# Two rests of the weights' split placed behind each chunk's shared results in VectorE's order

## Chip, cores and metric

The kernel runs on one core of a Trainium2 chip, in one launch. The metric is device time in microseconds (us), as the median of several runs. All shares and stamps below come from one profiled execution of the kernel before; its timeline counts from the start of its span.

## What is computed

Two layers of a residual trunk over an input x of 1 x 256 x 2048 in float32. Cut to what matters here:

```python
for l in range(2):
    h = rms_norm(x, pre_mix_norm[l])
    m = hybrid_mixer(h, ...)            # h @ w_in, 8 stick-breaking and 8 differential heads, @ w_o
    x = x + rms_norm(m, post_mix_norm[l])
    h = rms_norm(x, pre_ffn_norm[l])
    f = (silu(h @ w_gate[l]) * (h @ w_up[l])) @ w_down[l]   # 2048 -> 5632 -> 2048
    x = x + rms_norm(f, post_ffn_norm[l])
```

All weights are float32, and the output is compared at float32 accuracy.

## The kernel before

**Weights.** All weights are read once, in one order that is fixed on the host (`weights_in_turn`), as tiles of 128 x 1024 float32 (two blocks of 128 rows by 512 columns, 512 KB). To keep float32 accuracy with TensorE's faster 32-bit type, each tile is split: ScalarE writes a rounded copy `hi` (L271), VectorE writes the rest `lo = raw - hi` (L273), and every product is three matmuls, hi x hi, lo x hi, hi x lo (`product`, L976 to L978; the activations are split in the same way). In this text a *rest* is the operation on L273. `raw` tiles lie in a ring of 4 (L214), `hi` and `lo` in rings of 6. `feed` (L261) issues the split of the tiles in stream order, LOOKAHEAD = 4 tiles ahead of the product that uses them; `fetch` issues their loads on SP's queue, some tiles further ahead. A load into `raw` has to wait until the rest that read that slot four raw tiles earlier is done.

**Sevens.** Some pairs of weight tiles go through a seven-product scheme (as Strassen and Winograd's) instead of eight products: `seven_products` (L993). They need sums of weight blocks, made in `mixed_weights` (L229): the two tiles arrive as G and T (T with an accumulating second transfer issued from POOL, L224), T and G are combined on VectorE (L252, L253), and split on ScalarE (L245) and VectorE (L246) into hi, lo, Th and Tl. Four of the seven products are added into the output banks directly; four PSUM banks, p1, p6, p7 and q5, hold sums that several outputs share.

**Shared results.** After the last seven of a chunk, `shared_part` turns the four extra banks into four tiles, with one copy on ScalarE and four operations on VectorE:

```python
nc.scalar.copy(w[0], p1)                                                   # L1013
nc.vector.tensor_tensor(out=w[1], in0=p6, in1=w[0], op=ALU.subtract)       # L1014
nc.vector.tensor_tensor(out=w[2], in0=p7, in1=w[1], op=ALU.add)            # L1015
nc.vector.tensor_tensor(out=w[1], in0=q5, in1=w[1], op=ALU.add)            # L1016
nc.vector.tensor_tensor(out=w[3], in0=q5, in1=w[2], op=ALU.add)            # L1017
```

It is called in the input projection (L924), the output projection (L1066), gate and up (L1147) and down (L1242).

**Gate and up** (L1125 to L1166). 11 chunks of 512 columns in each layer; a chunk runs over 8 pairs of k blocks (kp) and adds into four banks c11, c12, c21, c22 (token half by gate or up). Four kps of a chunk are sevens (2, 4, 5, 6), but only two in chunk 0 (4, 6) and three in chunk 1 (4, 5, 6). In chunks 0 and 1 of each layer the sums of activations for later sevens are formed too (`pair_sums`, the f tiles of L1105, and `token_sums`, s, sh and sl, L983 to L990). The eight PSUM banks are two sets of four: the extra banks of a chunk are the output banks of the next one. So the first matmuls of chunk c + 1 into c11 to c22 must wait until the shared results of chunk c have read p1, p6, p7 and q5. At a chunk's end the banks are combined with the shared results and gated (L1152, L1153 silu on ScalarE, L1154, L1155), and the result is transposed on PE and copied back by ScalarE (L1161, L1162) some matmuls later.

**Down** (L1176 to L1270) runs in two halves of 1024 columns over 22 kps, seven of them sevens in each half; each half has one shared part. The last three kps of half 1 are done token half by token half.

**Order.** Engines run their queues in program order. The order of each queue is decided when the kernel is built, by a scheduler that places instructions by their dependencies and modelled readiness. `tc.issue_after(x)` adds an edge of order to it: what is issued inside stands behind x on the same engine. It adds no semaphore. Engines synchronise through semaphores on the tiles they share.

Of the kernel before, what the change touches and what calls it, by code (L numbers as in the profile page):

```python
# [2 lines left out]

# [6 lines left out]
F32 = mybir.dt.float32  # L10
# [3 lines left out]
ALU = mybir.AluOpType  # L14
# [7 lines left out]
NT = S // P  # L22
# [37 lines left out]
def gate_sevens(c):  # L60

    return (FIRST_SEVEN, NEXT_SEVEN)[c] if c < 2 else SEVEN
# [89 lines left out]
def kernel(  # L152
# [15 lines left out]
    nc = tc.nc  # L168
# [14 lines left out]
    def four_banks(odd, names):  # L183
        makers = (bank, bank, bank, last_bank) if odd else (acc_bank,) * 4
        return [make(n) for make, n in zip(makers, names)]
# [9 lines left out]
    def fetch(upto):  # L195
        while len(raws) < min(upto, len(stream)):
            i = len(raws)
            for j in range(i, min(i + EARLY + 1, mix_raw[3])):
                if j in sevens and j not in sums:
                    summed(j)  # L200
            if i in sevens:
                raws.append(sums[i])
                continue
            if i + 1 in sevens:
                g = mix_raw[0].tile([P, 2, CW], F32, tag="G", bufs=mix_raw[1], name=f"G{i}")
                loads.append(nc.sync.dma_start(g, stream[i]))
                raws.append(g)
                continue
            if i in own or i + 1 in own:
                raw = mix_pool[0].tile([P, 2, CW], F32, tag="v", bufs=2, name=f"V{i}")  # L210
            elif i in plain or i + 1 in plain:
                raw = mix_pool[0].tile([P, 2, CW], F32, tag="GU", bufs=4, name=f"GU{i}")
            else:
                raw = wpool.tile([P, 2, CW], F32, tag="raw", bufs=4, name=f"raw{i}")  # L214
            loads.append(nc.sync.dma_start(raw, stream[i]))
            raws.append(raw)
# [44 lines left out]
    def feed(upto):  # L261
        fetch(upto)
        while fed[0] < min(upto, len(stream)):
            i = fed[0]
            raw = raws[i]
            if i in sevens or i in plain or i in own:
                ready[i] = mixed_weights(i)
                fed[0] += 1
                continue
            hi = wpool.tile([P, 2, CW], F32R, tag="hi", bufs=6, name=f"hi{i}")  # L270
            nc.scalar.activation(hi, raw, AF.Copy)  # L271
            lo = wpool.tile([P, 2, CW], F32R, tag="lo", bufs=6, name=f"lo{i}")
            rest = nc.vector.tensor_tensor(out=lo, in0=raw, in1=hi.bitcast(F32), op=ALU.subtract)  # L273
            ready[i] = (hi, lo)
            fed[0] += 1
            rests.append(rest)

    rests = []

    def after_rests():  # L280

        return tc.issue_after(rests[-1].ins)
# [5 lines left out]
    def weights(i, ahead):  # L288
        feed(i + 1 + ahead)
        return ready[i]  # L290
# [175 lines left out]
    def start(gen, n=1):  # L466
        running.append([clock[0] + n, gen])
# [542 lines left out]
    def shared_part(extra, w):  # L1010

        p1, p6, p7, q5 = extra
        nc.scalar.copy(w[0], p1)  # L1013
        nc.vector.tensor_tensor(out=w[1], in0=p6, in1=w[0], op=ALU.subtract)  # L1014
        nc.vector.tensor_tensor(out=w[2], in0=p7, in1=w[1], op=ALU.add)  # L1015
        nc.vector.tensor_tensor(out=w[1], in0=q5, in1=w[1], op=ALU.add)  # L1016
        nc.vector.tensor_tensor(out=w[3], in0=q5, in1=w[2], op=ALU.add)  # L1017

    def shared_sign(t, col):
        return ALU.subtract if (t, col) == (1, 0) else ALU.add  # L1020
# [2 lines left out]
    for l in range(L):  # L1023
# [11 lines left out]
        mg = {}  # L1035
# [16 lines left out]
        for kp in LATE_O:  # L1052
            i, j = (plan[l]["o"][c, kp] for c in (2, 3))
# [4 lines left out]
            if kp == O_SEVEN[0]:  # L1058
                extra = four_banks(False, [f"{q}_o{l}" for q in ("p1", "p6", "p7", "q5")])
            hi, lo = weights(i, LOOKAHEAD)  # L1060
# [47 lines left out]
        def eight(banks, c, kp, toks, first, last):  # L1108
            g, u = weights(plan[l]["gate"][c, kp], LOOKAHEAD), weights(plan[l]["up"][c, kp], LOOKAHEAD)
            for kk in range(2):  # L1110
                st = xT[2 * kp + kk]
                for t in toks:
                    tick()
                    stat = (st[:, 0, t * P : (t + 1) * P], st[:, 1, t * P : (t + 1) * P])
                    for col, (hi, lo) in enumerate((g, u)):
                        product(banks[2 * t + col], stat, (hi[:, kk, :], lo[:, kk, :]), first and kk == 0, last and kk == 1)
# [8 lines left out]
        for c in range(FF // CW):  # L1125
            banks = four_banks(1 - c % 2, [f"c{q}_{l}_{c}" for q in ("11", "12", "21", "22")])
            mine = gate_sevens(c)
            order = FIRST_ORDER if c == 0 else tuple(range(KT // 2))
            if c == 0:
                for t in range(NT):  # L1130
                    for kp in order[:2]:
                        eight(banks, c, kp, (t,), kp == order[0], False)
                order = order[2:]
            extra = None
            for n, kp in enumerate(order):
                if (c, n) in FORM_AT:
                    with after_rests():
                        pair_sums(FORM_AT[c, n])
                if kp not in mine:
                    eight(banks, c, kp, range(NT), kp == 0, kp == order[-1])  # L1140
                    continue
                if kp == mine[0]:
                    extra = four_banks(c % 2, [f"{q}_{l}_{c}" for q in ("p1", "p6", "p7", "q5")])
                seven(banks, extra, c, kp, kp == mine[0], kp == mine[-1])
                if kp == mine[-1]:
                    w = [pool.tile([P, CW], F32, tag="t2", name=f"w{j}_{l}_{c}") for j in range(4)]
                    shared_part(extra, w)  # L1147
            at = pool.tile([P, 4, S], F32, tag="act", bufs=FF // CW, name=f"act{l}_{c}")
            act.append(at)
            sg = [w[0], w[2]]  # L1150
            for t, u in ((0, w[1]), (1, w[3])):
                nc.vector.tensor_tensor(out=sg[t], in0=banks[2 * t], in1=sg[t], op=shared_sign(t, 0))  # L1152
                nc.scalar.activation(sg[t], sg[t], AF.Silu, scale=rs[t][:, 0:1])  # L1153
                nc.vector.tensor_tensor(out=u, in0=banks[2 * t + 1], in1=u, op=ALU.add)  # L1154
                nc.vector.scalar_tensor_tensor(out=sg[t], in0=u, scalar=rs[t][:, 0:1], in1=sg[t], op0=ALU.mult, op1=ALU.mult)  # L1155

            def flip(sg=sg, at=at, c=c):
                for t in range(NT):
                    pb = (acc_bank if c % 2 else bank)(f"actT_ps{l}_{c}_{t}")
                    for j in range(4):  # L1160
                        nc.tensor.transpose(pb[:, j * P : (j + 1) * P], sg[t][:, j * P : (j + 1) * P], ident)  # L1161
                    nc.scalar.copy(at[:, :, t * P : (t + 1) * P], pb.rearrange("p (k q) -> p k q", k=4))  # L1162
                    yield 1

            start(flip(), DEFER_ACT)
# [7 lines left out]
        mg = {}  # L1173
        ssm = [small.tile([P, 4], F32, tag="ssm", name=f"ssm_d{l}_{t}") for t in range(NT)]
        nkp = FF // P // 2
        for half in range(2):  # L1176
# [48 lines left out]
            for kp in range(nkp - tail):  # L1225
                if half == 1 and kp == X_BACK:
                    back = [pool.tile([P, 4, S], F32, tag="act", bufs=FF // CW, name=f"xd{l}_{n}") for n in range(4)]
                    back = [b.rearrange("p k n -> p (k n)") for b in back]
                    xs[:] = [back[:2], back[2:]]
                    with in_turn():  # L1230
                        for t, h in ((0, 0), (0, 1), (1, 0), (1, 1)):
                            load_x(t, h, away[-1])
                if kp not in mine:
                    down(kp, range(NT))
                    continue
                if kp == mine[0]:
                    extra = four_banks(1 - half, [f"{q}_d{l}_{half}" for q in ("p1", "p6", "p7", "q5")])
                down_seven(kp)
                if kp == mine[-1]:
                    for t in range(NT):  # L1240
                        mg[t, half] = dn.tile([P, 2, CW], F32, tag="qk", bufs=4, name=f"mg_d{l}_{t}_{half}")
                    shared_part(extra, [mg[t, half][:, j, :] for t in range(NT) for j in range(2)])  # L1242
                    if open_sums[0]:
                        for c in cc:
                            nc.vector.tensor_tensor(out=accs[c, 1], in0=accs[c, 1], in1=mg[1, half][:, c % 2, :], op=shared_sign(1, c % 2))
# [5 lines left out]
            for t in range(NT):  # L1251
# [4 lines left out]
                for c in cc:  # L1256
                    for kp in range(nkp - tail, nkp):
# [3 lines left out]
                        hi, lo = weights(plan[l]["down"][c, kp], LOOKAHEAD)  # L1261
# [67 lines left out]
```

## Time and profile before

| what | value |
|---|---|
| runs | 2206.82, 2209.6, 2212.26 us; median 2209.6 us |
| profiled execution, own time | 2204.91 us |
| its span | 2203.2 us |
| granted TensorE clock | 0.999 |
| rests, L273 from raw | 522, 627.5 us busy, mean 1220 ns; idle before them 122.6 us, 121.4 of it put down to hi (L271) |
| hi, L271 from raw | 522, 541.1 us busy, mean 1053 ns; idle before them 234.8 us, 71.7 of it put down to the loads |
| loads of raw | 522 of 512 KB, 4.7 us median to landing |
| gate and up, from its first matmul to the first of down | 396.8 to 866.9 us in layer 0, 1493.4 to 1963.0 us in layer 1 |
| a steady gate and up chunk (6 to 7, layer 0) | 41.74 us |

The span runs from the first to the last instruction; the execution's own time is 1.7 us more. Busy shares are averages over the whole span, and stages differ. In a row of a timeline, the bracket at the end holds how long the engine stood idle before that instruction and what released it; idle time of an engine that nothing waits for costs nothing. PE stands for TensorE's matmuls, PEld for its weight loads, DVE for VectorE, ACT for ScalarE, POOL for GpSimd, SP for SyncE's queue of DMA issues.

### The profile page before, as it was taken

To read this page: it belongs to the slowest core of one execution; us is meant where nothing else is said; L and a number is where in the kernel's file an instruction comes from. 1 tells how busy PE (TensorE), PEld (TensorE's weight loads), DVE (VectorE), ACT (ScalarE), POOL (GpSimd) and SP (SyncE) were. 2 spreads that over 40 slices of the span, in tenths; PEclk is the share of its full clock that TensorE was granted. 3 is DMA by queue.
4 is the path that set the end of the run, shared out by engine and by line. 5 is a ranking of instruction groups with operands and counts; after the bars stand their busy time and mean duration, and the time that the engine had idled before them with its cause. 6 is when DMAs were issued, how large, how long until landed. Compare 5 with 4: busy or idle time off the path is not lost.

```text
span 2203.2 us, 28510 instructions
## 1 busy us (share of the span) xinstructions
PE 2180.6 (99%) x9991; PEld 1788.1 (81%) x9991; DVE 1902.2 (86%) x2609; ACT 1371.9 (62%) x2052; POOL 140.2 (6%) x186
## 2 busy tenths in 40 slices
PE   9999999999999999999999999999999999999998
PEld 7788888778888888888878888887788888888886
DVE  7888658899999999989888886579999999999897
ACT  7566665656656656666665666657566556566664
POOL 1200000000000000000011000000000000000000
PEclk9999999999999999999999999999999999999999
DMA  8654555776776675767465545658677677767683
GB/s 313 204 178 153 191 189 169 251 246 215 224 248 215 211 255 183 247 214 260 153 230 191 171 162 183 192 171 267 212 224 237 222 220 238 231 212 233 205 261 102
DMA packets 138512, 467.27 MB, mean 212 GB/s; under 512 B 15872, under 2 KB 16640, under 8 KB 137856
## 3 DMA queue, kind: packets, MB, share of 16 engines
q1 hardware_dynamic: 120656, 430.30, 56.5%
q0 software_dynamic: 15840, 28.84, 7.8%
q10 hardware_dynamic: 1872, 6.31, 0.8%
q8 instruction: 78, 1.28, 0.2%
q14 instruction: 66, 0.54, 0.1%
HBM read 457.00 MB, written 8.39 MB: 211 GB/s over the span
## 4 chain that ended last, share of the span: by engine, by line
PE 84%; DVE 9%; issue 2%; DMA 2%; ACT 2%; SPq 0%; DVEq 0%; ACTq 0%
PE c L976 8%; PE c L978 8%; PE c L977 8%; PE in L976 6%; PE in L978 6%; PE in L977 6%; PE dn L1212 4%; PE dn L1210 4%; PE dn L1209 4%; DVE lo L273 2%; PE p L977 2%; PE p L976 2%; PE p L978 2%; PE o L492 2%; PE o L493 2%
## 5 line engine op out<-in xcount | busy, mean ns | idle before, releaser
L273 DVE TENSOR_TENSOR lo<-raw,hi 128x1024 fp32r<-128x1024 f32 x522 | 627.5, 1220 | 122.6 <-ACT hi L271 121.4
L271 ACT ACTIVATE hi<-raw 128x1024 fp32r<-128x1024 f32 x522 | 541.1, 1053 | 234.8 <-DMA raw<-in_weights_in_turn_dram 71.7
L976 PE MATMUL c<-hi,xF 128*128 128x512 f32 x834 | 328.2, 396 | 3.5 <-DVE w L1017 1.6
L977 PE MATMUL c<-lo,xF 128*128 128x512 f32 x834 | 325.2, 390 | 0.5 <-DVE lo L273 0.5
L978 PE MATMUL c<-hi,xF 128*128 128x512 f32 x834 | 324.6, 390 | 0.0
L224 POOL DMA_DIRECT2D T<-in_weights_in_turn_dram x110 | 95.8, 874 | 1685.5 <-DMA T<-in_weights_in_turn_dram 596.5
L976 PEld LDWEIGHTS c<-hi,xF 128*128 128x128 f32 x834 | 156.3, 188 | 38.7 <-ACT hi L271 3.8
L977 PEld LDWEIGHTS c<-lo,xF 128*128 128x128 f32 x834 | 156.7, 188 | 33.5 <-DVE lo L273 2.7
L978 PEld LDWEIGHTS c<-hi,xF 128*128 128x128 f32 x834 | 156.6, 188 | 32.8
L1209 PE MATMUL dn<-hi,jh 128*128 128x512 f32 x432 | 168.3, 389 | 0.0
L1210 PE MATMUL dn<-lo,jh 128*128 128x512 f32 x432 | 168.1, 389 | 0.0
L273 DVE TENSOR_TENSOR lo<-G,hi 128x1024 fp32r<-128x1024 f32 x110 | 134.0, 1219 | 33.8 <-ACT hi L271 33.7
L245 ACT ACTIVATE Th<-G 128x1024 fp32r<-128x1024 f32 x110 | 116.0, 1055 | 40.2 <-DVE G L253 38.3
L246 DVE TENSOR_TENSOR Tl<-G,Th 128x1024 fp32r<-128x1024 f32 x110 | 134.0, 1218 | 5.3 <-ACT Th L245 5.3
L245 ACT ACTIVATE hi<-T 128x1024 fp32r<-128x1024 f32 x110 | 115.4, 1049 | 36.1 <-PE c L978 26.5
L246 DVE TENSOR_TENSOR lo<-T,hi 128x1024 fp32r<-128x1024 f32 x110 | 134.0, 1218 | 2.7 <-ACT hi L245 2.7
L253 DVE TENSOR_TENSOR G<-G,T 128x1024 f32<-128x1024 f32 x110 | 134.2, 1220 | 1.9
L1212 PE MATMUL dn<-hi,jl 128*128 128x512 f32 x432 | 133.0, 389 | 0.0
L245 ACT ACTIVATE Th<-T 128x512 fp32r<-128x512 f32 x110 | 68.9, 627 | 101.7 <-DVE T L252 85.5
L976 PE MATMUL in<-hi,xT 128*128 128x512 f32 x328 | 131.6, 402 | 0.0
L976 PE MATMUL in<-hi,xI 128*128 128x512 f32 x328 | 130.6, 401 | 0.0
L977 PE MATMUL in<-lo,xI 128*128 128x512 f32 x328 | 128.2, 391 | 1.5 <-DVE lo L273 1.5
(448 smaller groups left out, 4733.6 us busy)
## 6 DMA issues: line engine op xcount, KB each, us to landing
raw<-in_weights_in_turn_dram SPq DMA_DIRECT2D x522, 512.0 KB, 4.7
T<-in_weights_in_turn_dram SPq DMA_DIRECT2D x110, 512.0 KB, 4.5
G<-in_weights_in_turn_dram SPq DMA_DIRECT2D x110, 512.0 KB, 5.3
T<-in_weights_in_turn_dram POOLq DMA_DIRECT2D x110, 256.0 KB, 6.9
GU<-in_weights_in_turn_dram SPq DMA_DIRECT2D x32, 512.0 KB, 4.6
V<-in_weights_in_turn_dram SPq DMA_DIRECT2D x8, 512.0 KB, 3.9
away_ffn<-x ACTq DMA_DIRECT2D x8, 512.0 KB, 4.1
xd<-away_ffn SPq DMA_DIRECT2D x8, 512.0 KB, 8.1
```

What stands on the lines that cost most here:

```text
L224: nc.gpsimd.dma_start(sums[i][:, 0, :], stream[i - 1][:, 0, :], accum_op=ALU.add)
L245: nc.scalar.activation(h, w, AF.Copy)
L246: nc.vector.tensor_tensor(out=l, in0=w, in1=h.bitcast(F32), op=ALU.subtract)
L253: nc.vector.tensor_tensor(out=g, in0=g, in1=t2.unsqueeze(1).to_broadcast([P, 2, CW]), op=ALU.add)
L271: nc.scalar.activation(hi, raw, AF.Copy)
L273: rest = nc.vector.tensor_tensor(out=lo, in0=raw, in1=hi.bitcast(F32), op=ALU.subtract)
L976: nc.tensor.matmul(a, sh, hi, start=first, stop=False, skip_group_check=open_sums[0])
L977: nc.tensor.matmul(a, sh, lo, start=False, stop=False, skip_group_check=open_sums[0])
L978: nc.tensor.matmul(a, sl, hi, start=False, stop=last, skip_group_check=open_sums[0])
L1209: nc.tensor.matmul(accs[c, t], sh, hi[:, kk, :], start=first, stop=False, skip_group_check=open_sums[0])
L1210: nc.tensor.matmul(accs[c, t], sh, lo[:, kk, :], start=False, stop=False, skip_group_check=open_sums[0])
L1212: nc.tensor.matmul(accs[c, t], sl, hi[:, kk, :], start=False, stop=last, skip_group_check=open_sums[0])
```

## The change

`shared_part` returns its last operation on VectorE (w[3]). In gate and up and in down, that operation is kept together with a count of 2, and the next two rests that `feed` issues on plain raw or G tiles are put behind it by `tc.issue_after`. The calls in the input and the output projection keep nothing. There are 26 such places, 11 in each gate and up and 2 in each down.

```diff
-            rest = nc.vector.tensor_tensor(out=lo, in0=raw, in1=hi.bitcast(F32), op=ALU.subtract)
+            with behind():
+                rest = nc.vector.tensor_tensor(out=lo, in0=raw, in1=hi.bitcast(F32), op=ALU.subtract)
...
+    held = [None, 0]
+
+    def behind():
+
+        if held[1] == 0:
+            return nullcontext()
+        held[1] -= 1
+        return tc.issue_after(held[0].ins)
...
-        nc.vector.tensor_tensor(out=w[3], in0=q5, in1=w[2], op=ALU.add)
+        return nc.vector.tensor_tensor(out=w[3], in0=q5, in1=w[2], op=ALU.add)
...
-                    shared_part(extra, w)
+                    held[:] = shared_part(extra, w), 2
...
-                    shared_part(extra, [mg[t, half][:, j, :] for t in range(NT) for j in range(2)])
+                    held[:] = shared_part(extra, [mg[t, half][:, j, :] for t in range(NT) for j in range(2)]), 2
```

The lines of the changed kernel are shifted: the rests are on L274 and the shared results on L1022 to L1026 there, the end of a chunk on L1161 to L1164.

No instruction is added or removed on any engine. In a steady chunk VectorE's order is, before: rest, L1014, L1015, rest, L1016, L1017, L1152; after: L1014, L1015, L1016, L1017, rest, rest, L1152. Around it the scheduler places some other instructions differently: loads on SP's queue (a T load ahead of one raw load, a raw load ahead of one G load in each steady chunk), a few operations of ScalarE in chunks 0 and 1, the transposes of chunk 10 on PE (28 matmuls earlier), and, at the end of layer 1's down, six matmuls of another sum that now stand ahead of those whose rests are held.

More of the change, by code (lines that the diff above doesn't have):

```diff
@@ L1 @@
 import math
-from contextlib import ExitStack
+from contextlib import ExitStack, nullcontext
 import concourse.bass as bass
```

## Prediction

> **What bounds the kernel now.** I read the page's busy line first, then PE's waits in the gate and up stage, then stretches of 41 to 42 us, then VectorE's, ScalarE's and PE's timelines around the shared results.
>
> ```profile
> PE 2180.6 (99%) x9991; PEld 1788.1 (81%) x9991; DVE 1902.2 (86%) x2609; ACT 1371.9 (62%) x2052; POOL 140.2 (6%) x186
> ```
>
> PE is busy for 99% of the span; an edit on VectorE can only win where PE waits for it. The windows view (stretch and its length, then busy us of PE, PEld, DVE, ACT, POOL, then granted clock, DMA share, GB/s) shows where: chunks 0 to 1 and 1 to 2 of layer 0, and a steady chunk, 6 to 7.
>
> ```profile
> 444.00:485.00 41.00, 40.77 (x181) 32.82 (x180) 39.09 (x52) 24.84 (x30) 3.45 (x4) 1.00 0.72 221
> 485.00:527.00 42.00, 39.78 (x175) 31.65 (x175) 38.61 (x43) 26.35 (x30) 2.61 (x3) 1.00 0.74 226
> 652.06:693.80 41.74, 41.74 (x190) 34.58 (x189) 39.00 (x44) 25.35 (x29) 3.48 (x4) 1.00 0.73 233
> ```
>
> PE is never idle in the steady chunk; it is a little in the first two. The waits of PE from 436 to 530 us (us, times, longest):
>
> ```profile
> PE p L977 <- DVE Tl L246: 1.2, 3, 0.5
> PE c L976 <- DVE w L1017: 0.8, 1, 0.8
> PE c L976 <- DVE w L1015: 0.5, 1, 0.5
> PE p L976 <- ACT Th L245: 0.2, 1, 0.2
> ```
>
> The same view answers with no line at all for 530 to 862, 860 to 1085 and 1626 to 1958 us. For 1532 to 1626 (layer 1's first chunks) it gives nearly the same sum, 2.7 us. A wait also stretches the matmul behind it. Matmuls start 0.227 us apart when nothing is late; what the trace has over that is 4.7 us in 444 to 527 and 4.3 us in 1540 to 1623. So **9.0 us, 0.4% of the time, is all that the change can win in gate and up**.
>
> The place itself, chunk 1 to 2 of layer 0, on VectorE and ScalarE (start, duration, instruction, idle time before it and its releaser):
>
> ```profile
> 483.47 0.68 DVE L1014 TENSOR_TENSOR w<-p,w 128x512 f32<-128x512 f32 x1
> 487.86 1.23 DVE L273 TENSOR_TENSOR lo<-raw,hi 128x1024 fp32r<-128x1024 f32 x1 [3.71 <-ACT hi L271]
> 489.00 0.68 DVE L1015 TENSOR_TENSOR w<-p,w 128x512 f32<-128x512 f32 x1
> 489.61 0.68 DVE L1152 TENSOR_TENSOR w<-c,w 128x512 f32<-128x512 f32 x1
> 490.20 0.68 DVE L1016 TENSOR_TENSOR w<-q,w 128x512 f32<-128x512 f32 x1
> 490.80 0.68 DVE L1017 TENSOR_TENSOR w<-q,w 128x512 f32<-128x512 f32 x1
> 491.40 1.21 DVE L273 TENSOR_TENSOR lo<-raw,hi 128x1024 fp32r<-128x1024 f32 x1
> 492.53 0.68 DVE L1154 TENSOR_TENSOR w<-c,w 128x512 f32<-128x512 f32 x1
> ```
>
> ```profile
> 486.77 1.06 ACT L271 ACTIVATE hi<-raw 128x1024 fp32r<-128x1024 f32 x1 [7.66 <-DMA raw<-in_weights_in_turn_dram]
> 489.67 1.06 ACT L271 ACTIVATE hi<-raw 128x1024 fp32r<-128x1024 f32 x1 [1.84 <-DMA raw<-in_weights_in_turn_dram]
> ```
>
> The first rest stands ahead of L1015 and waits 3.71 us for a late raw tile. L1015 to L1017 stand behind it, and PE needs their banks: it waits at 489.74 for L1015, then for L1017, then for Tl:
>
> ```profile
> 491.53 0.50 PE L976 MATMUL c<-hi,xF 128*128 128x512 f32 x1 [0.81 <-DVE w L1017]
> 504.42 0.50 PE L977 MATMUL p<-Tl,sh 128*128 128x512 f32 x1 [0.54 <-DVE Tl L246]
> ```
>
> **The change, part by part.** No instruction is added or removed. 26 shared results (22 gate and up, 4 down) each hold two rests of 1.22 us (L273: 627.5 us over 522) behind the last of four operations of 0.68 us. Only orders move, as the lists of instructions of each engine show; no instruction waits on a further semaphore. What stands behind the two rests on VectorE is L1152 or L1154 of the chunk's end, and what waits for a rest is PE and, through the slot of its raw tile, SP's queue.
>
> *Steady chunks, 16 of them.* Before, one rest stands between w1 and w2's successors and waits 0.28 us for hi:
>
> ```profile
> 693.79 0.68 DVE L1014 TENSOR_TENSOR w<-p,w 128x512 f32<-128x512 f32 x1
> ...
> 709.08 1.22 DVE L246 TENSOR_TENSOR Tl<-G,Th 128x1024 fp32r<-128x1024 f32 x1
> 712.39 1.23 DVE L273 TENSOR_TENSOR lo<-G,hi 128x1024 fp32r<-128x1024 f32 x1 [2.08 <-ACT hi L271]
> ```
>
> p6 is complete at 693.27. After: L1014 at 693.33, L1015 694.05, L1016 694.77, L1017 to 696.05, the two rests to 698.25. L1152 stood at 698.07, so +0.18 us on VectorE, and the 2.08 us of idle time at 712 takes that up. PE uses the later rests' tiles from 705.58, 7 us after they end. Their raw slots come free up to 3.2 us later (697.1 for 693.87), but the tiles that load there landed at 700.73 and 703.17 and are first read at 724.72 and 726.28. Behind them on SP's queue one T load changes places with a raw load (708.06 and 707.46) and the next raw with a G (710.71 and 710.33): 0.6 us for tiles that are read over 10 us after they land. Sum 0; without that cover it would be 16 x 0.18 = 2.9 us. (The Trainium skill, Perfetto Trace Analysis, "Identifying the Most-Contended Engine", would judge TensorE by its weight loads, 81% here, and optimise the engine with the highest occupancy, which makes VectorE with 86% the bound. The trace disagrees: no PE wait from 530 to 862. As a rival it stands below.)
>
> *Chunk 0 to 1, layer 0.* Both rests move behind L1017 and the operations on f (L1105). L1015 to L1017 come about 0.9 us earlier, where PE didn't wait. The first rest ends at 448.1 instead of 445.3, so the load into its raw slot is issued 2.8 us later, at 448.1 (it took 5.35 us). PE waited at 457.46 (0.2 over) for a rest behind that load: hi 1.06, sh 0.61, sl 0.69 and the rest's own 1.22 are 3.6, with some 0.4 for the handovers 4.0, so 448.1 + t + 4.0. Break-even is t = 5.4 if PE is to stand as before, 5.2 to win the 0.2. The nearest raws took 4.33 (449.52) and 5.96 (436.91), mean 5.1: 457.2. I take -0.1; bounds -0.2 and (t = 5.96) +0.6.
>
> *Chunk 1 to 2, layer 0.* L1017 ends at 486.3 instead of 491.4, so PE's waits at 489.74 (0.61 over its spacing) and 491.53 (0.98) go. But the second rest still waits for its raw tile (hi at 489.67, DMA of 8.25 us): it runs 490.76 to 491.9, and L1154 starts at 492.5 as before. Everything behind on VectorE (Tl, for which PE waits at 504.42, 0.70 over, and at 526.21, 0.57) stands still, so PE, early by 1.6, waits there longer instead: what PE gains over the whole is what VectorE gains, and VectorE hangs on that DMA. I take 0; bounds 0 and -1.6.
>
> *Layer 1's first chunks.* The same two places. In chunk 0 to 1 the first rest (1539.88) leaves the front of L1015 and ends at about 1544.3 instead of 1541.1; the load behind it took 6.95 us. PE waited at 1554.17 (0.68 over): 1544.3 + t + 3.95 is 1553.35 with t = 5.1, so that wait goes, -0.7; with 6.95 it is 1555.2, +1.0. In chunk 1 to 2 the second rest's hi is ready at 1586.34 and the rest stood at 1587.54, behind L1015 to L1017; held, it runs at 1586.37, and VectorE is 1.17 us early from there on. PE's waits there are 0.99, 0.71 and 0.55 (1587.68, 1600.56, 1622.35); as PE can't be earlier than VectorE at the last, 1.2 is the whole of the layer: -0.7 and -0.5. Bounds +1.0 and -4.3, all of its waits.
>
> *Down, 4 places.* Half 0: VectorE saves up to 1 us of a 1.32 us idle where PE doesn't wait: 0. Half 1 of layer 0: the held rest ends at about 1084.1 (1080.25 and 3.86 of shared results and rests) for a use at 1084.26: 0, or +0.3. End of layer 1: six matmuls change places and an accumulator ends 1.36 us later, in front of 1.59 us idle before L512's next: 0.
>
> **Sum**: -0.1 + 0 - 1.2 + 0 = -1.3 us. The profiled execution took 2204.91 us (span 2203.2 and 1.7 around it), 4.7 below the median 2209.6 of the runs. It would become 2203.6, and the median 2209.6 - 1.3 = **2208.3 us**. A measurement of this kernel can tell about 0.3%, 6.6 us, from no change.
>
> **Rivals.**
> *All PE waits of the first chunks go* (faster): VectorE, freed from waiting at the head of its queue, arrives in time for Tl as well. For it: the waits stand exactly where the moved rests stood, and the runs are up to 7 us longer than the profile, so they may hold more of these waits. Against: hi at 489.67 is set by the DMA. Time: 2209.6 - 9.0 = 2200.6.
>
> *The raw slots come free too late* (slower): a rest that is held keeps its raw tile up to 3.2 us longer, SP's queue stops at the load that needs the slot, and G, T and the later raws queue behind it. It decides from t = 5.4 us (layer 0) and 5.9 us (layer 1), where the sums above cross 457.46 and 1554.17. For it: this answer on the line that issues them (us to landing).
>
> ```profile
> DMA to landing us min/median/max: 3.1/4.7/10.6
> ```
>
> Around 483.6 four loads close together took 7.6 to 9.4 us. At 9.4 both layers lose: 448.1 + 9.4 + 4.0 = 461.5 against 457.46, +4.0; 1557.65 against 1554.17, +3.5; together +7.5, 2217.1. Against: the median is 4.7, and fewer loads are under way while one is held.
>
> *VectorE is the bound* (the rule above, worked out from the rows): each steady chunk is 0.18 us longer, 16 x 0.18 = +2.9, so 2212.5, slower but not measurably.
>
> *Nothing moves* where it counts, since each late operation waits for a DMA: 2209.6.
>
> **How the numbers follow.** Forecast (about -1.3) 0.47; all waits go 0.24; raw slots 0.20; VectorE the bound 0.05; nothing 0.04. Faster by over 0.3% is 0.24, slower 0.20, within 0.47 + 0.05 + 0.04 = 0.56. The range runs from 2200.0, just beyond the first rival's time, to 2216.0, just short of the second's 2217.1. The forecast's own bounds are -0.2 - 1.6 - 4.3 = -6.1 and +0.6 + 1.0 + 0.3 = +1.9: 2203.5 to 2211.5.
>
> **What would show it.** Right: L1014 to L1017 in a row in each gate and up chunk; no PE wait for L1015 or L1017's successors at 489 to 492; Tl waits there as long or longer (1.2 becomes up to 2.8); steady chunks of 41.74 us; the raw load of 445.3 issued some 2.8 us later. Wrong: PE waits between 530 and 862, a Tl wait that vanishes, or the rests at 457 and 1554 later than before by over 1 us.

## The result and the profile after

The changed kernel takes 2204.53 us (median of 14 runs, 2201.59 to 2210.04) where the kernel before takes 2209.13 (14 runs): ratio 0.9982, 95% interval 0.9973 to 0.9990, that is -2.2 to -6.0 us. A second set of runs (below) gave 0.9993, 0.9984 to 1.0002. The mean of the two, 0.9988, is about -2.8 us, less than the 0.3% of the prediction's bound. (The ratios are not quotients of the medians, which differ a little: 0.9979 in the first set. This text goes by the ratios.) The forecast was 2208.3 us, in a range from 2200.0 to 2216.0. The profiled execution went from a span of 2203.2 to 2201.9 us, the 1.3 us that were forecast; but that agreement is partly luck: chunks 1 and 2 of the two layers lost 2.1 us between these two profiles, and the rest of the span grew by 0.8.

The page's busy line, and the same three stretches of the windows view, after:

```profile
PE 2179.0 (99%) x9991; PEld 1788.0 (81%) x9991; DVE 1903.6 (86%) x2609; ACT 1370.9 (62%) x2052; POOL 140.5 (6%) x186
```

```profile
444.00:485.00 41.00, 40.63 (x182) 32.91 (x181) 39.59 (x53) 24.86 (x29) 3.46 (x4) 1.00 0.72 212
485.00:527.00 42.00, 39.95 (x180) 32.33 (x179) 38.47 (x43) 26.24 (x30) 2.61 (x3) 1.00 0.78 234
652.06:693.80 41.74, 41.74 (x190) 34.58 (x189) 38.99 (x43) 24.84 (x29) 3.49 (x4) 1.00 0.76 228
```

The steady chunk has the same 190 matmuls in 41.74 us and PE is never idle in it; all eight steady chunks together take 333.97 us in layer 0 and 333.87 in layer 1, before and after. In the first two stretches PE gets through 1 and 5 matmuls more (182 for 181, 180 for 175). PE's waits in 436 to 530 us are now these:

```profile
PE p L985 <- ACT Th L245: 1.5, 1, 1.5
PE p L986 <- DVE Tl L246: 1.2, 3, 0.6
```

The waits for the shared results (L1015 and L1017 before) are gone. Their sum is not: 2.7 us before and after. They went to Th, which had 0.2 before; Tl kept its 1.2. (In layer 1, 1532 to 1626 us, the sum fell from 2.7 to 2.0.) VectorE's timeline at the end of chunk 1 of layer 0 shows how:

```profile
483.64 0.68 DVE L1023 TENSOR_TENSOR w<-p,w 128x512 f32<-128x512 f32 x1
484.42 0.69 DVE L1024 TENSOR_TENSOR w<-p,w 128x512 f32<-128x512 f32 x1
485.15 0.69 DVE L1025 TENSOR_TENSOR w<-q,w 128x512 f32<-128x512 f32 x1
485.75 0.68 DVE L1026 TENSOR_TENSOR w<-q,w 128x512 f32<-128x512 f32 x1
487.66 1.23 DVE L274 TENSOR_TENSOR lo<-raw,hi 128x1024 fp32r<-128x1024 f32 x1 [1.22 <-ACT hi L271]
490.93 1.23 DVE L274 TENSOR_TENSOR lo<-raw,hi 128x1024 fp32r<-128x1024 f32 x1 [2.04 <-ACT hi L271]
492.07 0.68 DVE L1161 TENSOR_TENSOR w<-c,w 128x512 f32<-128x512 f32 x1
492.67 0.68 DVE L1163 TENSOR_TENSOR w<-c,w 128x512 f32<-128x512 f32 x1
```

The four operations stand in a row and are done at 486.4, 5 us sooner. VectorE then waits for the same two late raw tiles as before, now in 1.22 and 2.04 us, and starts the first addition into c12 (L1163) at 492.67, where the old order had it at 492.53.

**Four stretches of each layer.** From the starts of PE's matmuls in each trace I measured, in chunks 1 and 2: A, first matmul of chunk 1 (some stand between the last ones of chunk 0) to its first into p1; B, from there to the first of chunk 2; C, from there to its first p1; D, from there to the first of chunk 3. Layer 0 / layer 1, us:

| kernel | A | B | C | D |
|---|---|---|---|---|
| before | 30.65 / 31.18 | 20.22 / 20.24 | 13.68 / 13.07 | 31.48 / 31.51 |
| c0, same order | 31.28 / 31.68 | 20.19 / 20.20 | 12.80 / 13.58 | 31.52 / 31.49 |
| e2, chunks 2 to 10 held | 32.13 / 30.97 | 20.21 / 20.21 | 13.38 / 13.12 | 31.47 / 31.47 |
| e3, down held | 31.14 / 31.42 | 20.19 / 20.24 | 15.96 / 13.73 | 30.22 / 31.47 |
| after | 30.10 / 30.11 | 20.76 / 20.46 | 11.80 / 11.81 | 32.62 / 32.28 |
| a1, same order as after | 30.12 / 30.07 | 20.46 / 21.59 | 11.80 / 11.83 | 34.46 / 31.35 |
| e1, chunks 0 and 1 held | 30.11 / 30.07 | 20.13 / 20.35 | 11.80 / 11.83 | 32.24 / 33.05 |
| g1, chunk 0 held | 30.07 / 30.08 | 20.36 / 20.74 | 12.54 / 12.89 | 31.61 / 31.24 |
| g2, chunk 1 held | 32.07 / 31.23 | 20.21 / 20.18 | 11.83 / 11.80 | 32.71 / 32.78 |
| f1, after with a swap undone | 31.41 / 31.99 | 19.93 / 19.95 | 11.83 / 11.80 | 30.51 / 30.23 |
| e5, behind the whole end | 30.11 / 30.12 | 20.18 / 20.10 | 17.34 / 13.90 | 30.23 / 30.68 |
| e6, behind the additions | 30.05 / 30.11 | 20.19 / 21.14 | 11.81 / 11.80 | 31.10 / 30.25 |

A falls by 1.3 us in layer 0 (mean of five without the hold at chunk 0, 31.45, to four with it, 30.10) and by 1.2 in layer 1 (31.30 to 30.08). B + C + D together stay: 65.17 without the hold at chunk 1 and 65.21 with it in layer 0, 65.04 and 64.83 in layer 1. The sum is -2.7 us, which agrees with the -2.8 of the runs. B + C + D of single profiles lie between 64.2 and 66.7, so a change of some tenths of a us there would not be seen.

### The profile page after: what moved, and what is told of

Read it like the earlier page. It is cut to its first block, busy times and chain, and to the rows that moved or that the text cites. A ratio compares the mean times of both kernels' runs of the same rounds, so it can differ in the third digit from the quotient of the medians.

```text
span 2201.9 us, 28532 instructions
## 1 busy us (share of the span) xinstructions
PE 2179.0 (99%) x9991; PEld 1788.0 (81%) x9991; DVE 1903.6 (86%) x2609; ACT 1370.9 (62%) x2052; POOL 140.5 (6%) x186
## 4 chain that ended last, share of the span: by engine, by line
PE 88%; DVE 6%; ACT 2%; DMA 2%; issue 1%; SPq 0%; DVEq 0%; ACTq 0%
PE c L987 9%; PE c L986 9%; PE c L985 9%; PE in L985 6%; PE in L987 6%; PE in L986 6%; PE dn L1221 4%; PE dn L1218 4%; PE dn L1219 4%; PE p L986 2%; PE p L985 2%; PE p L987 2%; PE o L502 2%; PE o L501 2%; PE o L503 2%; DVE lo L274 2%
## 5 line engine op out<-in xcount | busy, mean ns | idle before, releaser
L274 DVE TENSOR_TENSOR lo<-raw,hi 128x1024 fp32r<-128x1024 f32 x522 | 626.0, 1220 | 115.2 <-ACT hi L271 114.5
L987 PEld LDWEIGHTS c<-hi,xF 128*128 128x128 f32 x834 | 156.5, 188 | 32.7
L274 DVE TENSOR_TENSOR lo<-G,hi 128x1024 fp32r<-128x1024 f32 x110 | 134.0, 1218 | 29.5 <-ACT hi L271 29.5
```

What stands on the lines that cost most here:

```text
L987: nc.tensor.matmul(a, sl, hi, start=False, stop=last, skip_group_check=open_sums[0])
```

## The experiments

**c0: no hold, the old order with the new text.**

```diff
-                    held[:] = shared_part(extra, w), 2
+                    held[:] = shared_part(extra, w), 0
```

(the same in down)

> The changed kernel with no rest held anywhere (counts of 0); every engine's order is that of the kernel before. It measures the noise, and gives a second profile of the old order. Any theory of the change: 2209.1 us, within 2 us of the kernel before. If the profile of before was a lucky execution (2204.9 where its runs lie at 2206.8 to 2212.3), this profile is longer and shows in which stage the other 4 us are: theory A (waits in chunks 0 to 2) then has more than 9.0 us over the 0.227 us spacing of the matmuls there; theory B (waits in steady chunks) has PE waits between 530 and 862 us.

Measured: 0.9999 (0.9990 to 1.0008), as expected. Its profile has a span of 2209.4 us against 2203.2, and PE's longest wait in 430 to 530 us is this one (3.0 us in two waits, 2.8 the longer), at 434.7 us, before the first shared results:

```profile
PE p L985 <- ACT Th L245: 3.0, 2, 2.8
```

and no PE wait between 530 and 862. Of the 6.2 us, 5.2 are in stretches that the change doesn't touch: 2.7 ahead of chunk 1's first matmul in layer 0 and 2.5 at the start of layer 1's input projection. So one profile of this kernel may differ by more than the change is worth, in stages with late loads; stretches compared over several profiles say more than two spans.

**e1, e2, e3: parts of the change alone.**

```diff
+ held[:] = shared_part(extra, w), 2 if c < 2 else 0       # e1
+ held[:] = shared_part(extra, w), 2 if c >= 2 else 0      # e2
+ held[:] = shared_part(extra, w), 0                       # e3; down as in the change
```

In e1 and e2 down holds nothing.

> Held only in chunks 0 and 1 of gate and up of each layer. Theory A (all of the gain is waits of PE in the first chunks of both layers): the whole gain, -4.6 us, 2204.5. Theory B (the 3.3 us beyond the predicted 1.3 come from steady chunks): -1.3, 2207.8. Theory C (they come from another place, down or the layer boundary): -1.3 as well.

> Held only in chunks 2 to 10 of gate and up of each layer. Theory A: 0, 2209.1, and steady chunks of 41.74 us as before. Theory B: -3.3, 2205.8. Theory C: 0. If VectorE were the bound: +2.9, 2212.

> Held only in down. Theory A: 0, 2209.1. Theory B: 0. Theory C (the end of layer 1, the layer boundary): -3.3, 2205.8, with a shorter stretch from the end of down of layer 0 to the first product of layer 1's input projection, or from the last shared results to the end.

Measured: e1 0.9992 (0.9983 to 1.0001), e2 1.0002 (0.9993 to 1.0011), e3 1.0004 (0.9995 to 1.0013). Neither the steady chunks nor down win or lose anything that these times can tell (their intervals reach from -1.5 to +2.9 us), and in e2's profile chunks 3 to 10 take 41.7 to 41.8 us each like everywhere. e1's time alone doesn't tell -1.3 from -2.8, nor from 0, but its stretches A to D are those of the changed kernel. Theory A stands; its -4.6 was too much.

**a1: the change again, with a count of 1.** The scheduler puts the second rest behind the results on its own, so that a count of 1 gives the order of a count of 2 on every engine.

```diff
-                    held[:] = shared_part(extra, w), 2
+                    held[:] = shared_part(extra, w), 1
```

> The change with a count of 1 instead of 2: the order of every engine is that of the changed kernel, so it is a second profile and a second set of times of it. Theory A (PE's waits in chunks 1 and 2 of both layers, which the profile of before shows smaller than most executions have them): -3.3 to -4.6 us against before, and from the first matmul of chunk 1 to the first of chunk 3 about 94.8 us in layer 0 and 95.0 in layer 1, where the old order has 96.6 and 96.4. Theory C (the rest of the gain is elsewhere or noise): -1.3 us.

Measured: 0.9993 (0.9984 to 1.0002), that is -1.5 us: beside theory C's -1.3, with an interval (-3.5 to +0.4) that just reaches theory A's -3.3. A to D add up to 96.84 in layer 0 and 94.84 in layer 1, against 96.63 and 96.40 in the mean of before, c0, e2 and e3: layer 0 won nothing in this profile, since its D was 34.46.

**g1, g2: chunk 0 alone, chunk 1 alone.**

```diff
+ held[:] = shared_part(extra, w), 2 if c == 0 else 0      # g1
+ held[:] = shared_part(extra, w), 2 if c == 1 else 0      # g2
```

> Held only at chunk 0 of each layer. Theory now: the change wins about 1.2 us a layer in the first third of chunk 1 (first matmul of chunk 1 to its first p1: 30.65 to 32.13 us in four profiles of the old order, 30.07 to 30.12 in three of the new) and next to nothing from the hold at chunk 1, since what it wins there is given back at Th and Tl in chunk 2. So -2.4 us against before; the first third at 30.1, the stretch from chunk 2's first matmul to chunk 3's as in the old order (12.8 to 16 and 30.2 to 31.5). Rival (each hold wins on its own): -1.2 us.

> Held only at chunk 1 of each layer. Theory now: -0.2 us against before, 0 within the noise; the first third of chunk 1 at about 31.3 as in the old order; the stretch in chunk 2 up to its first p1 at 11.8 instead of 13 to 16, and the rest of chunk 2 longer by the same (32 to 34 instead of 31.2). Rival: -1.5 to -3.7 us, if the 1.6 to 2.2 us a layer won up to the first p1 are kept.

Measured: g1 0.9990 (0.9982 to 0.9999), -2.2 us; g2 1.0003 (0.9994 to 1.0011). Both as the theory had them. In g2, C falls to 11.8 and D grows to 32.7: what the hold at chunk 1 wins before p1 is lost behind it. As far as these intervals tell, the whole gain is the hold at chunk 0.

**f1: one swap undone.** With the hold at chunk 0 the scheduler also places the rest of tile 149 (541 in layer 1) ahead of sl, the split of the pair sums. This kernel holds the rests as in the change, but puts that one behind sl again:

```diff
+        if fed[0] in (149, 541):
+            return tc.issue_after(formed["0_5" if fed[0] == 149 else "1_5"].ins)
...
-        nc.vector.tensor_tensor(out=sl, in0=s, in1=sh.bitcast(F32), op=ALU.subtract)
+        formed[nm] = nc.vector.tensor_tensor(out=sl, in0=s, in1=sh.bitcast(F32), op=ALU.subtract)
```

> The changed kernel with one thing undone in chunk 1 of each layer: the rest of tile 149 (541 in layer 1) stands behind sl of the pair sums again, as in the old order; the rests held behind the shared results stay held. Theory now (the 1.2 us a layer come from this rest, which PE waited for at 457.46 and 1554.17, having been put ahead of sl, which waits for sh behind a hi whose load is late): the first third of chunk 1 is back at 30.7 to 32 us, and the gain over before falls from 2.6 to about 0.2 us. Rival (it comes from the shared results being earlier, or from other loads): 30.1 us as in the changed kernel, gain 2.6 us.

Measured: 0.9981 (0.9972 to 0.9989), a miss in the time and right in the stretch. A is back at 31.41 and 31.99. VectorE in the changed kernel, then in f1, then PE in f1:

```profile
453.22 2.35 DVE L274 TENSOR_TENSOR lo<-raw,hi 128x1024 fp32r<-128x1024 f32 x2
456.88 0.69 DVE L999 TENSOR_TENSOR sl<-s,sh 128x512 fp32r<-128x512 f32 x1 [1.30 <-ACT sh L997]
457.49 2.35 DVE L274 TENSOR_TENSOR lo<-raw,hi 128x1024 fp32r<-128x1024 f32 x2
```

```profile
453.09 1.22 DVE L274 TENSOR_TENSOR lo<-raw,hi 128x1024 fp32r<-128x1024 f32 x1
456.25 0.69 DVE L1003 TENSOR_TENSOR sl<-s,sh 128x512 fp32r<-128x512 f32 x1 [1.94 <-ACT sh L1001]
456.86 3.49 DVE L274 TENSOR_TENSOR lo<-raw,hi 128x1024 fp32r<-128x1024 f32 x3
```

```profile
458.13 0.50 PE L990 MATMUL c<-lo,xF 128*128 128x512 f32 x1 [1.05 <-DVE lo L274]
```

Two rests stand ahead of sl in the changed kernel and one in f1; the second one (tile 149) then waits while VectorE stands idle for sh, and PE waits 1.05 us for it (1.58 for tile 541). The kernel before has the same order; the three rests behind sl are 149 to 151:

```profile
453.36 1.22 DVE L273 TENSOR_TENSOR lo<-raw,hi 128x1024 fp32r<-128x1024 f32 x1
455.57 0.69 DVE L990 TENSOR_TENSOR sl<-s,sh 128x512 fp32r<-128x512 f32 x1 [0.99 <-ACT sh L988]
456.19 3.49 DVE L273 TENSOR_TENSOR lo<-raw,hi 128x1024 fp32r<-128x1024 f32 x3
```

This is where a part of the gain of A comes from, and not all of it. PE's wait for this rest is longer in f1 than in any profile of the old order (0.03 to 0.57 us), so A is back at its old length for more than the old reason. What PE's matmuls in A start late by, over their spacing, has three parts in the mean of the five profiles without the hold at chunk 0: 0.6 us in layer 0 and 0.8 in layer 1 at this rest; 0.3 and 0.25 at the transposes of chunk 0, which wait for the last multiplication of that chunk's end; and 0.3, in layer 0 alone, at the first matmul into the bank that L1015 reads. g2's waits of PE in 436 to 532 us hold two of them:

```profile
PE actT_ps L1170 <- DVE w L1164: 0.6, 1, 0.6
PE c L986 <- DVE lo L274: 0.4, 1, 0.4
```

All three are gone in the six profiles that have the hold at chunk 0 and tile 149's rest ahead of sl. In f1 only the first is back. The new order of ScalarE in chunk 0, where each silu stands ahead of a hi that it stood behind before, can explain the second; it wasn't tried by itself.

But f1's edge moved more than the swap: further on, in chunk 1, SP's queue has tile 162's raw load ahead of a G and a T load and the three raw loads after it ahead of another G, rests 158 and 159 and a hi change places, and so do 28 matmuls of that chunk on PE. The raw tile of rest 163 landed at 487.99 instead of 489.73, and D fell to 30.51 and 30.23. So f1 lost 1.3 and 1.9 us in A and won about 2 in D. Which of the moved instructions won it wasn't tried by itself.

**e5, e6: fill VectorE's wait at the end of chunk 1.** Two rests are fed two tiles later and held behind the chunk's end: e5 behind all six operations, e6 behind the four additions only.

```diff
+HOLD_BACK = ((1, KT // 2 - 1),)
...
+            ahead = LOOKAHEAD - 2 if (c, kp) in HOLD_BACK else LOOKAHEAD
...
+            if (c, KT // 2 - 1) in HOLD_BACK:
+                held[:] = done, 2
+                feed(plan[l]["up"][c + 1, 1] + 1)
+                for t, u in ((0, w[1]), (1, w[3])):
+                    nc.vector.scalar_tensor_tensor(out=sg[t], in0=u, scalar=rs[t][:, 0:1], in1=sg[t], op0=ALU.mult, op1=ALU.mult)
```

This is e6: `done` is its last addition, and the two multiplications come behind the two rests. In e5 `done` is the last multiplication, and the last three lines are not there.

> The change, and in chunk 1 of each layer the next two rests stand behind the six operations of the chunk's end too (they are fed two tiles later). Theory A in its second half, that what PE wins at the chunk's end is given back at Tl in chunk 2 because the second rest waits for its raw tile ahead of the chunk's end: VectorE does those 3.4 us of work while it would wait (1.2 and 2.0 us idle in the profile after), Tl comes up to 2.3 us sooner, PE's waits for Tl and Th in chunk 2 go: -1.2 to -2.3 us a layer against the changed kernel, 2200 to 2202 us. Rival (Tl waits for the T and G transfers themselves): same as the changed kernel, 2204.5. Rival (the first rest then comes too late for PE): slower than it, 2206 or more.

> The changed kernel, and at chunk 1 of each layer the two rests stand behind the four additions of the chunk's end as well, but ahead of the two multiplications that wait for silu (the earlier try put them behind those too, and PE waited 3.4 us for the first rest). VectorE does 2.4 us of additions in the 1.2 and 2.0 us in which it waits for the raw tiles, and is about 2.0 us ahead at the first operation on T. Theory now (PE's waits for Th and Tl in chunk 2 hang on VectorE's work behind the late second rest): those waits shrink by 1.2 to 2 us in layer 0 and 0.7 to 1.3 in layer 1, the rest of chunk 2 at 30.2 to 31.2 us instead of 32 to 34; -2 to -3 us against the changed kernel, about -5 against before. Rival (Tl hangs on the T and G loads): as the changed kernel.

Measured: e5 1.0000 (0.9991 to 1.0008), no better than before. The rival with the late first rest was right, for a reason that I had not seen: the multiplications wait for silu, which stands on ScalarE behind the hi of the late tile, so VectorE stood idle for 5.63 us and PE waited 3.4 us for the first rest; C is 17.34. (The late tile's hi ran at 491.98 here, 2.2 us later than in the changed kernel; that is in the 5.63.) PE's waits in 436 to 535 us:

```profile
PE c L987 <- DVE lo L275: 3.4, 1, 3.4
PE p L987 <- DVE Tl L247: 0.3, 1, 0.3
```

That what followed was then quicker (D 30.23) bears the theory out.

e6 0.9969 (0.9958 to 0.9981), 2200.36 us, -6.8 us: faster than the kernel before, and by more than was expected. It is also some 4 us faster than the changed kernel (0.9969 against the mean of 0.9988, a difference of 0.0019 with about 0.0013 of uncertainty), though its interval overlaps with that of the changed kernel's first set. VectorE there, from the first addition:

```profile
485.42 0.68 DVE L1163 TENSOR_TENSOR w<-c,w 128x512 f32<-128x512 f32 x1
...
487.22 0.68 DVE L1165 TENSOR_TENSOR w<-c,w 128x512 f32<-128x512 f32 x1
487.82 1.21 DVE L275 TENSOR_TENSOR lo<-raw,hi 128x1024 fp32r<-128x1024 f32 x1
490.49 1.23 DVE L275 TENSOR_TENSOR lo<-raw,hi 128x1024 fp32r<-128x1024 f32 x1 [1.46 <-ACT hi L272]
```

The additions fill what was idle; 1.46 us of waiting are left of 3.26, and D is 31.10 and 30.25. Only 5 runs stand behind this ratio.

**r3: three raw slots instead of four,** in both orders.

```diff
-                raw = wpool.tile([P, 2, CW], F32, tag="raw", bufs=4, name=f"raw{i}")
+                raw = wpool.tile([P, 2, CW], F32, tag="raw", bufs=3, name=f"raw{i}")
```

> The kernel before with 3 slots for raw tiles instead of 4, so that loads start later and more rests find their tile late. It is slower than before; how much is not forecast. It is to be compared with the next run.

> The changed kernel with 3 slots for raw tiles. Theory A (a late raw tile stops VectorE ahead of the shared results in the old order, and not in the new): faster than the old order with 3 slots, by more than the 4 us that it wins with 4 slots. The rival of the prediction (a held rest keeps its slot, so that loads start too late): slower than the old order with 3 slots, since each held slot is now one of three.

Measured: old order 1.0047 (1.0032 to 1.0062), new order 1.0028 (1.0018 to 1.0038). With a slot less both are slower, and the new order is not the worse one: 2212.78 against 2216.98 us, 4.2 us less. The intervals overlap, so that "by more than with 4 slots" is open; the rival of the held slots is not borne out. Nor does the pair show theory A: A to D differ by 0.9 us between the two profiles, both layers together, and the spans by 9.8, mostly elsewhere.

## Why the prediction was right, and where it was wrong

- **All that can be won is 9.0 us of PE waits; steady chunks 0.** Right for the steady chunks. Chunks 3 to 10 took 41.7 to 41.8 us in every profile with four slots, the changed order of VectorE in them had no price, and e2 gave 1.0002. VectorE as the bound (+2.9) falls: it would have had 16 longer chunks, and there was none. (It is the engine that the Trainium skill's rule in Perfetto Trace Analysis, "Identifying the Most-Contended Engine", would have optimised first.) The 9.0 us were read from one profile; A to D are 0.6 and 0.4 us longer in the mean of four.
- **Chunk 0 to 1, -0.1 in layer 0 and -0.7 in layer 1.** This step failed in layer 0 and was too small in layer 1. I took PE's waits at 457.46 and 1554.17 for waits on the rest behind the freed raw slot (tiles 150 and 542). They were for the rest one tile earlier (149 and 541), whose raw tile was long there and which stood behind sl. The list of instructions that I had showed that rest moved ahead of sl, and I gave it no value. It is worth about half of the gain of A in layer 0 and two thirds in layer 1; the transposes and, in layer 0, the bank of L1015, where I had written that PE didn't wait, are most of the rest. The load into the freed slot was issued at 448.26, 2.9 us later, as forecast (445.33 before), and took 5.38; its rest ended at 458.7, later than the 457.5 that my sum gives for that t, but PE first read it at 461.8. Measured: -1.3 and -1.2. Of the -1.3, only 0.55 could be read from the profile that I had (30.65 to 30.10): it was the quickest of the five in this stretch.
- **Chunk 1 to 2, 0 in layer 0.** Right, with its stamps: L1017's end 486.3 forecast, 486.4 found; second rest 490.76 and 490.93; L1154 492.5 and 492.67; a wait for Th took the place of those for the shared results, where I had named Tl, whose waits kept their 1.2. Over the profiles B + C + D changed by 0.04. In layer 1, -0.5 forecast, -0.2 found, which is within the scatter of the profiles. That "VectorE hangs on that DMA" was half of it: e6 won some 4 us more with the order of the loads left alone, by putting work into the wait. One sign was not met: L1014 to L1017 stand in a row in 20 of the 22 chunks, and in chunk 0 of each layer L1152 still stands among them.
- **Down, 0.** Right: e3 gave 1.0004, and from layer 1's first matmul of down to the end it is 240.25 us before and 240.32 after.
- **All waits go (2200.6).** Not so: the sum of PE's waits in 436 to 530 stayed at 2.7 us, and in layer 1 2.0 of 2.7 were left.
- **Raw slots too late (2217.1).** Its price was put on the wrong tile: with the first use of tile 150 at 461.8 a load would have to take some 3 us more than the 5.4 that it took before PE waits at all.
- **The sum.** -1.3 us forecast, about -2.8 measured (-2.2 to -6.0 in one set, -3.5 to +0.4 in the other). Of the 1.4 us that are missing, the first layer's A is 1.2 and the second's 0.5; chunk 1 to 2 of layer 1 gave 0.3 less than forecast.

## To carry to other kernels

On an in-order queue, ask for each instruction that waits for a transfer what stands behind it that could run now, and put that ahead: here the shared results first, and then the additions too (e6, some 4 us more, in five runs). Before a wait is priced, look up which tile the waiting instruction reads; two rests that follow each other on one line differ by a load. And an edge of order moves other instructions than the one it names: list them, and price each one that stands beside a wait.

## What I had not expected

Profiles of one order differed by 6.2 us in their span (2203.2 and 2209.4) at nearly the same clock (0.999 and 0.998), most of it in two stretches: 8.9 and 11.6 us for the same matmuls ahead of chunk 1, 49.2 and 51.7 at the start of layer 1, while the steady chunks repeated within 0.05 us.
